# Products without use in TensorE's waits: norms, RWKV projections and latent attention of a two-block network

## The chip, the cores and the metric

One core of one Trainium2 chip runs the whole kernel. The metric is the device time of one execution in microseconds (us); the time quoted is the median of several runs. A profiled execution is a single one, and its trace gives when each instruction ran on each engine: TensorE (PE; its weight loads PEld), VectorE (DVE), ScalarE (ACT), GpSimd (POOL) and the queue that issues most transfers (SP). The trace also gives the TensorE clock that was granted: 1.00 stands for 2.4 GHz, 0.50 for 1.2 GHz, and a value between is a mean over a stretch in which both occurred.

## The reference, cut to what matters

256 tokens of 1024 features (and 256 context tokens) pass through two networks in float32. The first has two layers: a mixer of neighbourhood attention and mLSTM, an MLP, an RWKV-7 mixer, an MLP. The second has two layers of SwiGLU, a mixer (the second one is multi-head latent attention), cross attention to a memory, SwiGLU. The parts that the change touches:

```python
def rms_norm(x, eps=NORM_EPS):
    xf = x.astype(jnp.float32)
    return (xf * lax.rsqrt(jnp.mean(xf * xf, axis=-1, keepdims=True) + eps)).astype(x.dtype)
...
def rwkv_prepare(h, mu, w_rkv, w0, w1, w2, a0, a1, a2, g1, g2, k_k, k_a):
    xx = centred_shift(h) - h
    xr, xw, xk, xv, xa, xg = h[None] + xx[None] * mu[:, None, None, :]
    r, k, v = jnp.einsum('sbtd,sde->sbte', jnp.stack([xr, xk, xv]), w_rkv)
...
def _mla_mixer(h, positions, w_in, q_lora_g, kv_lora_g, w_uq, w_ukv, q_g, k_g, w_out):
    c_q, c_kv, k_r = jnp.split(h @ w_in, [MLA_Q_LORA, MLA_Q_LORA + MLA_KV_LORA], axis=-1)
    q = (_rmsnorm(c_q, q_lora_g) @ w_uq).reshape(b, s, MLA_HEADS, MLA_QK)
    kv = (_rmsnorm(c_kv, kv_lora_g) @ w_ukv).reshape(b, s, MLA_HEADS, MLA_NOPE + MLA_V)
```

## The kernel before, in words

Weights and activations are kept with features on the 128 partitions. Each float32 weight tile is split on the fly into a rounded part (`wh`, by ACT) and a remainder (`wl`, by DVE), and each product is the sum of two or three matmuls (`mm2`, lines 166 to 171; `mm3`, lines 159 to 164). Most of the time TensorE works through such products without a break.

**Norms.** The sum of squares of x is gathered by ACT and DVE (`sumsq`, L262) or ACT and POOL (`pre_norm`, L530), reduced over the partitions by two small matmuls (`rstd_from`, L280), raised to the power -1/2 by POOL (L259), and spread over the partitions again by two matmuls against a diagonal (`bcast_tok`, L290). In `modulate` (L1464) and `rwkv_in` (L2067) these matmuls come ahead of the products that use the norm; in `mla_mixer` (L894) the scale is applied later, but the small matmuls still stand ahead of the products. `modulate` is called with one stream (`len(xs) == 1`) in one place only, the MLP of the first network's second layer (`mlp`, L1964, with `ns == 1`).

**Order of the work.** Outside the planned parts the framework orders the instructions of each engine by itself. Three parts are ordered by hand with a planner, `Weave` (L321): `rwkv_in`, the RWKV scan (`rwkv_scan`, L2561) and `mla_mixer`. Each piece of work is a generator that announces an engine and an estimated duration before it issues instructions (`yield "PE", 0.43`); the planner lets the generators run in the order of estimated start and rank, and that order is what each engine's queue gets. Resources such as PSUM banks are slots that are taken and given back (`take`, `give`): "G" are the four banks pG of the large products, "L" the banks pL of the small ones.

**Warm products.** The planner can put matmuls of the identity with itself, whose output nobody reads, into TensorE's queue. Before each PE piece it adds up what its plan holds for TensorE in the window that ends with this piece, and if that is under the share `DUTY` it adds products ahead of the piece (`keep`, L419). A fourth value of a PE request says what share of its duration counts as load; without it, all of it counts:

```python
    def keep(self, end, work, after=None):
        need = self.DUTY * self.WINDOW - self.load(end) - work
        if need > 0:
            n = math.ceil(need / 0.107)
            self.add_warm(end if after else max(self.free.get("PE", 0.0), end - self.WINDOW), min(n, 4) if after else n, after)
```

One unit of n is 64 columns, up to four units make one matmul call of 256 columns, and the plan's time for PE is moved on by 0.107 us for each unit. Before the change only the scan does this (`rw_warm`, L2751, into a bank pX of its own; `rw_heat`, L2761, 12 such calls ahead of its first work). In `rwkv_in` (L2087) and `mla_mixer` (L944) the line `w.FILL = w.DUTY = 0.0` turns it off.

**rwkv_in** (L2067). After the norms, a front makes the shifted and mixed inputs on DVE, ACT and POOL (`ri_front`, `ri_mix`), and `ri_products` runs the products k, w, a, g, r and v through the banks pG. While r and v run, `ri_items` and `ri_unit` work out decay, a, kk and so on for 8 blocks of features in 2 directions, each with small PE pieces: `ri_low` (L2402, L2403), the spread of kk's scale (L2452) and the sum for the bonus (L2531). The sums of squares of k (L2276) and their transposition (L2359) belong here too. DVE, ACT and POOL work alongside, and SP stores and loads pieces in DRAM.

**mla_mixer** (L894). Products "in", "uq", "ukv" and "out" (`ml_tokens`, `ml_main`) go through pG; norms, rotations, transposes (L1109, L1158, L1232) and attention per head lie between them, and the products of the next stage (`ml_memory`) fill in.

## Time and profile before

| | |
|---|---|
| median of 3 runs | 2817.14 us (2816.12 to 2821.49) |
| the profiled execution, its own time | 2816.91 us |
| span of its trace, first to last instruction | 2814.8 us |
| mean granted TensorE clock over the span | 0.966 |
| PE busy | 2623.0 us (93%) |
| DVE busy | 1898.6 us (67%) |
| ACT busy | 1353.7 us (48%) |
| POOL busy | 401.0 us (14%) |
| chain that ended last | PE 74%, DVE 15%, ACT 4%, POOL 2%, DMA 2% |

The first line is what is to be predicted. The trace describes the profiled execution alone, and its span leaves out about 2 us of start and end. "Busy" of PE counts matmuls at either clock, so that a matmul at 1.2 GHz counts twice as long as the same one at 2.4 GHz. The stages that the change touches lie at 783 to 1057 us (`rwkv_in`), 1373 to 1563 us (the MLP with one stream) and 2361 to 2520 us (`mla_mixer`).

### The profile page before, as it was taken

What the parts mean: (1) busy time and instruction counts of PE and PEld (TensorE: products, weight loads), DVE (VectorE), ACT (ScalarE), POOL (GpSimd) and SP (SyncE); (2) the same over time, 40 slices, a digit from 0 to 9 for tenths busy, and PEclk for the clock granted to TensorE, in tenths of its full rate; (3) what the DMA queues carried; (4) which work ended last, traced back from release to release, by engine and by line L of the source; (5) the groups of instructions that cost most, each with busy time, mean ns of one, the idle gap of its engine ahead of it and who ended that gap; (6) DMA issues with size and microseconds to landing.
All of it is one profiled execution on the core that took longest, in us unless ns stands there. A gap on an engine that the chain in (4) does not pass through costs nothing.

```text
span 2814.8 us, 47376 instructions
## 1 busy us (share of the span) xinstructions
PE 2623.0 (93%) x18980; PEld 2193.8 (78%) x18980; DVE 1898.6 (67%) x3252; ACT 1353.7 (48%) x2548; POOL 401.0 (14%) x396
## 2 busy tenths in 40 slices
PE   6999999999979988886899999999999999799999
PEld 4977667888857675775688888988888888788887
DVE  4463667544376884986785787876876776765884
ACT  3344333223245550676454554554654554664563
POOL 1210100000043552234100101001101001311100
PEclk9999999999988899999899999999999999999999
DMA  7244445533222666232355455533555555233454
GB/s 278 75 158 148 143 150 194 180 120 106 90 73 94 213 226 158 64 81 88 123 195 193 166 182 197 184 124 115 180 190 185 180 190 180 83 121 120 167 193 150
DMA packets 108122, 425.93 MB, mean 151 GB/s; under 512 B 14334, under 2 KB 50430, under 8 KB 66046
## 3 DMA queue, kind: packets, MB, share of 16 engines
q1 hardware_dynamic: 107326, 420.76, 44.3%
q8 instruction: 149, 2.44, 0.4%
q10 hardware_dynamic: 576, 2.15, 0.2%
q14 instruction: 71, 0.58, 0.1%
HBM read 397.68 MB, written 24.13 MB: 150 GB/s over the span
## 4 chain that ended last, share of the span: by engine, by line
PE 74%; DVE 15%; ACT 4%; POOL 2%; issue 2%; DMA 2%; SPq 0%; POOLq 0%; ACTq 0%; DVEq 0%
PE g L170 17%; PE g L171 9%; PE g L162 8%; PE g L163 7%; PE g L164 7%; PE a L170 6%; PE a L171 3%; DVE pr L2736 2%; DVE N L2738 2%; PE pG L162 2%; PE pG L163 2%; PE pG L164 2%; PE d L1405 1%; PE pX L2754 1%; DVE wl L72 1%
## 5 line engine op out<-in xcount | busy, mean ns | idle before, releaser
L72 DVE TENSOR_TENSOR wl<-raw,wh 128x1024 fp32r<-128x1024 f32 x512 | 627.6, 1226 | 359.7 <-ACT wh L71 356.8
L71 ACT CAST wh<-raw 128x1024 fp32r<-128x1024 f32 x512 | 537.1, 1050 | 631.8 <-PE g L170 259.1
L170 PE MATMUL g<-xnh,wh 128*128 128x512 f32 x800 | 287.3, 399 | 5.4 <-DVE xnh L200 5.4
L170 PE MATMUL a<-xnh,wh 128*128 128x512 f32 x704 | 251.9, 397 | 0.0
L170 PE MATMUL g<-hh,wh 128*128 128x512 f32 x704 | 246.6, 396 | 0.0
L171 PE MATMUL g<-xnh,wl 128*128 128x256 f32 x800 | 224.0, 280 | 0.0
L171 PE MATMUL a<-xnh,wl 128*128 128x256 f32 x704 | 197.0, 280 | 0.0
L171 PE MATMUL g<-hh,wl 128*128 128x256 f32 x704 | 196.4, 279 | 0.0
L547 POOL TENSOR_TENSOR acc<-acc,sq 128x256 f32<-128x256 f32 x63 | 65.7, 1042 | 839.9 <-ACT sq L546 561.9
L170 PEld LDWEIGHTS g<-xnh,wh 128*128 128x128 f32 x800 | 150.7, 188 | 42.7 <-DVE xnh L200 4.6
L170 PEld LDWEIGHTS a<-xnh,wh 128*128 128x128 f32 x704 | 132.6, 188 | 31.6
L170 PEld LDWEIGHTS g<-hh,wh 128*128 128x128 f32 x704 | 132.1, 188 | 31.8
L171 PEld LDWEIGHTS g<-xnh,wl 128*128 128x128 f32 x800 | 151.3, 189 | 0.1
L2754 PE MATMUL pX<-ident 128*128 128x256 f32 (+3 forms) x388 | 103.8, 378 | 35.5 <-DVE N L2738 19.2
L163 PE MATMUL g<-wl,hh 128*128 128x256 f32 x448 | 129.3, 289 | 6.6 <-DVE wl L72 6.6
L162 PE MATMUL g<-wh,hh 128*128 128x256 f32 x448 | 131.8, 295 | 3.3 <-ACT wh L71 3.1
L171 PEld LDWEIGHTS a<-xnh,wl 128*128 128x128 f32 x704 | 133.0, 189 | 0.1
L171 PEld LDWEIGHTS g<-hh,wl 128*128 128x128 f32 x704 | 132.6, 188 | 0.0
L164 PE MATMUL g<-wh,hl 128*128 128x256 f32 x448 | 128.5, 287 | 0.0
L259 POOL TENSOR_TENSOR rs<-ms,mhalf 128x2 f32<-128x2 f32 (+2 forms) x53 | 56.5, 1067 | 426.6 <-DVE ms L257 426.5
L2754 PEld LDWEIGHTS pX<-ident 128*128 128x128 f32 x388 | 64.8, 201 | 55.9 <-DVE N L2738 28.8
L162 PE MATMUL g<-hh,wh 128*128 128x512 f32 x256 | 101.1, 397 | 1.5 <-ACT hh L1485 1.5
(635 smaller groups left out, 6995.3 us busy)
## 6 DMA issues: line engine op xcount, KB each, us to landing
raw<-in_w_mlp SPq DMA_DIRECT2D x64, 1024.0 KB, 4.8
raw<-in_w_ada SPq DMA_DIRECT2D x48, 1024.0 KB, 6.4
raw<-in_w_pre_gu SPq DMA_DIRECT2D x44, 1024.0 KB, 4.8
raw<-in_w_post_gu SPq DMA_DIRECT2D x44, 1024.0 KB, 4.8
raw<-in_w_pre_down SPq DMA_DIRECT2D x22, 1024.0 KB, 4.8
raw<-in_w_post_down SPq DMA_DIRECT2D x22, 1024.0 KB, 4.8
raw<-in_w_ab SPq DMA_DIRECT2D x14, 1024.0 KB, 4.9
d_bk<-h SPq DMA_DIRECT2D x16, 512.0 KB, 3.0
```

The lines of the kernel that those rows point to most:

```text
L71: nc.scalar.copy(h[:, :w], r)
L72: nc.vector.tensor_tensor(l[:, :w], r, h[:, :w].bitcast(F32), op=ALU.subtract)
L162: mm(ps, wh, xh, start=start, stop=False)
L163: mm(ps, wh, xl, start=False, stop=False)
L164: mm(ps, wl, xh, start=False, stop=stop)
L170: mm(ps, wh, x, start=start, stop=False)
L171: mm(ps[:, 0], wl, x[:, 0], start=False, stop=stop)
L259: nc.gpsimd.tensor_tensor(rs[:, :n], ms[:, :n], self.mhalf[:, :n], op=ALU.pow)
L547: nc.gpsimd.tensor_tensor(acc, acc, sq, op=ALU.add)
L2736: nc.vector.tensor_tensor(pr, bc(N[:, k + 1 :, k], 2, k), bc(N[:, k, :k], 1, m), op=ALU.mult)
L2738: row = nc.vector.tensor_tensor(N[:, k + 1 :, :k], N[:, k + 1 :, :k], pr, op=ALU.add)
L2754: mm = self.nc.tensor.matmul(o, self.ident, bc(self.ident[:, :64], 1, cols // 64), start=True, stop=True)
```

## The change

A method `idle_products` issues n products of the identity with itself into a PSUM tile that nobody reads. It is called in three norms: 6 products in `mla_mixer` ahead of `rstd_from`; 4, 3 and 7 in `modulate` with one stream, ahead of `rstd_from`, ahead of `bcast_tok` and behind it; 7 and 3 in `rwkv_in`, ahead of `rstd_from` and of `bcast_tok`. In the plans of `rwkv_in` and `mla_mixer` DUTY becomes 0.55 (FILL stays 0), with `wv_warm` as the routine that issues a product: it writes into the bank pG that was handed back last, if the plan has one free at that time, and issues nothing otherwise. `rwkv_in` also gets 12 products of 256 columns at the start of its plan (`wv_heat`). Five PE pieces of `rwkv_in` get another planned duration, and a share of it that counts as load: L2276, L2359, `ri_low`, L2452 and L2531.

```diff
+    def idle_products(self, n):
+        o = self.pst.tile([P, 512], F32, name="t")[:, :T]
+        for _ in range(n):
+            self.nc.tensor.matmul(o.rearrange("p (n t) -> p n t", t=64), self.ident, bc(self.ident[:, :64], 1, 4), start=True, stop=True)
...
+    def wv_warm(self, cols, after=None):
+        now = self.weave.free.get("PE", 0.0)
+        free = [q for at, q in self.weave.slots["G"] if at <= now]
+        if free:
+            o = self.pG[free[-1]][:, :cols].rearrange("p (n t) -> p n t", t=64)
+            self.nc.tensor.matmul(o, self.ident, bc(self.ident[:, :64], 1, cols // 64), start=True, stop=True)
+
+    def wv_heat(self, n):
+        for _ in range(n):
+            yield "PE", 0.427, 0.0
+            self.wv_warm(256)
...
                 self.xn = xh, xl, acc = self.pre_norm(pn, self.vec("mix_norm", 1))
+                self.idle_products(6)
                 self.rs = self.rstd_from(acc, D)
...
                     w = self.weave = Weave(G=4, T=2, S=1, A=1, tmp=2, rop=1, sc=5, pT=4, mq=2, mj=1)
-                    w.FILL = w.DUTY = 0.0
+                    w.FILL, w.DUTY, w.warm = 0.0, 0.55, self.wv_warm
...
         accs = self.sumsq(ph.pools["acc"], [lambda k, x=x: x[:, k] for x in xs], KT)
         more(steps[0])
+        idle = (4, 3, 7) if len(xs) == 1 else (0, 0, 0)
+        if idle[0]:
+            self.idle_products(idle[0])
         rs = [self.rstd_from(acc, D) for acc in accs]
         more(steps[1])
+        if idle[1]:
+            self.idle_products(idle[1])
         rbs = [self.bcast_tok(r, ph.pools["rb"]) for r in rs]
-
+        if idle[2]:
+            self.idle_products(idle[2])
         more(steps[2])
...
-            w.FILL = w.DUTY = 0.0
+            w.FILL, w.DUTY, w.warm = 0.0, 0.55, self.wv_warm
             rm = self.rm = self.phase("rm", acc=2, rb=2, c=1)
             rm.__enter__()
             accs = self.sumsq(rm.pools["acc"], [lambda k, x=x: x[:, k] for x in self.xs], KT)
+            self.idle_products(7)
             rs = [self.rstd_from(acc, D) for acc in accs]
+            self.idle_products(3)
             rbs = [self.bcast_tok(r, rm.pools["rb"]) for r in rs]
...
             w.add(self.ri_rest(enter), 0)
+            w.add(self.wv_heat(12), -1)
...
-            yield "PE", 0.8
+            yield "PE", 0.8, 0.15, 0.2
             for t in range(4):
                 nc.tensor.matmul(self.pK[:, t * 16 + 2 * n : t * 16 + 2 * n + 2], self.os[q][:, t * P : (t + 1) * P], self.hm, start=True, stop=True)
...
-            yield "PE", 0.4
+            yield "PE", 0.7, 0.15, 0.2
             for t in range(4):
                 nc.tensor.matmul(self.pM[r, t * P : (t + 1) * P], rn[:, 16 * t : 16 * t + 16], self.ident, start=True, stop=True)
...
-        yield "PE", 0.43
+        yield "PE", 0.9, 0.15, 0.7
         nc.tensor.matmul(self.pL[g], lr["w"][:, c], lr["h"][z], start=True, stop=False)
...
-            yield "PE", 0.85
+            yield "PE", 0.55, 0.15, 0.15
             nc.tensor.matmul(self.pL[g], self.sel[r, k % 2], self.rT[r], start=True, stop=True)
...
-        yield "PE", 0.4
+        yield "PE", 0.4, 0.15, 0.2
         for t in range(2):
             c = z * 32 + t * 16
             nc.tensor.matmul(self.pM[:, c + k : c + 16 : KT], a[:, t * P : (t + 1) * P], self.hmk[:, k], start=True, stop=True)
```

## Rows read from the trace of the kernel before

**Rows 1.** Windows: the stages touched. Columns as in the head line.
```profile
core 0: us, PE busy (x) PEld busy (x) DVE busy (x) ACT busy (x) POOL busy (x), PEclk, DMA share, GB/s
783.00:833.00 50.00, 29.76 (x112) 23.32 (x112) 44.34 (x62) 23.70 (x41) 24.34 (x20) 0.77 0.15 53
875.00:1057.00 182.00, 161.50 (x879) 128.02 (x879) 145.59 (x183) 97.92 (x160) 97.43 (x96) 0.83 0.55 187
1373.00:1563.00 190.00, 182.49 (x1028) 158.37 (x1028) 134.68 (x213) 95.48 (x149) 0.71 (x1) 0.96 0.53 182
2361.00:2520.00 159.00, 138.72 (x1045) 128.15 (x1044) 109.54 (x273) 92.64 (x216) 39.37 (x25) 0.96 0.35 109
```

**Rows 2.** Windows: five stretches of rwkv_in at the low clock.
```profile
879.00:892.00 13.00, 12.38 (x55) 11.72 (x55) 10.73 (x22) 7.85 (x15) 8.03 (x6) 0.51 0.15 64
897.50:905.50 8.00, 7.23 (x27) 4.52 (x27) 2.14 (x6) 2.27 (x5) 0.00 (x0) 0.57 0.27 115
929.70:939.60 9.90, 9.73 (x20) 4.83 (x21) 9.87 (x11) 5.96 (x11) 7.21 (x8) 0.50 0.58 211
959.60:972.60 13.00, 13.00 (x35) 7.83 (x35) 11.69 (x14) 4.95 (x8) 7.10 (x9) 0.52 0.51 179
...
1024.00:1032.00 8.00, 7.74 (x31) 6.12 (x31) 6.21 (x8) 4.08 (x6) 5.06 (x6) 0.57 0.85 252
```

**Rows 3.** Timeline, PE, rwkv_in: start, us, line, tiles, shape [idle before <- releaser].
```profile
786.40 1.87 PE L280 MATMUL t<-ones,acc 128*128 128x1 f32 x8 [3.61 <-DVE acc L273]
788.92 2.07 PE L290 MATMUL t<-dg,ones 128*128 128x128 f32 x8 [0.66 <-DVE dg L289]
798.29 0.80 PE L162 MATMUL pG<-mh,wh 128*128 128x512 f32 x1 [7.30 <-ACT mh L2201]
...
898.27 1.56 PE L2359 MATMUL pM<-ident,rn 128*16 128x128 f32 x8 [3.35 <-ACT o L2361]
```

**Rows 4.** Timeline, PE, the scan: products of the kind added, 256 columns.
```profile
1341.04 1.56 PE L2754 MATMUL pX<-ident 128*128 128x256 f32 x6
```

**Rows 5.** Timeline (two rows), source L2531 and groups of ACT from 925 to 1048.
```profile
893.98 0.50 PE L2402 MATMUL pL<-lhw,lww 128*128 128x512 f32 x1
894.41 0.50 PE L2403 MATMUL pL<-llw,lww 64*128 64x512 f32 x1
...
L2531 PE MATMUL pM<-hmk,xx x52: 165/251/373, 953.9 to 1051.2; 128*128 128x2 f32 x52
...
L2302 ACT COPY o<-pG 128x512 f32<-128x512 f32 (+1 forms) x14 | 6.6, 488 | 9.6 <-PE pG L164 9.6
```

**Rows 6.** Timeline, PE, the norm of the MLP with one stream.
```profile
1375.17 0.61 PE L280 MATMUL t<-ones,acc 128*128 128x1 f32 x4 [2.07 <-DVE acc L273]
1377.14 1.22 PE L290 MATMUL t<-dg,ones 128*128 128x128 f32 x4 [1.36 <-DVE dg L289]
1381.62 0.80 PE L170 MATMUL g<-x,wh 128*128 128x512 f32 x1 [3.26 <-ACT wh L71]
...
1384.42 0.63 PE L170 MATMUL g<-x,wh 128*128 128x512 f32 x1
...
1390.18 0.40 PE L170 MATMUL g<-x,wh 128*128 128x512 f32 x1
...
1390.53 0.40 PE L170 MATMUL g<-x,wh 128*128 128x512 f32 x1
```

**Rows 7.** Latent attention: two rows of the PE timeline, two windows.
```profile
2364.47 0.61 PE L280 MATMUL t<-ones,acc 128*128 128x1 f32 x4 [2.60 <-POOL acc L547]
...
2414.89 1.09 PE L1158 MATMUL pT<-ident,qn 128*96 128x128 f32 x4 [3.75 <-DVE qn L1085]
...
2366.40:2369.70 3.30, 3.30 (x18) 3.30 (x17) 0.34 (x2) 0.39 (x1) 0.57 (x1) 0.50 0.93 327
2414.80:2421.00 6.20, 6.11 (x29) 6.03 (x30) 2.34 (x6) 1.37 (x2) 0.00 (x0) 0.50 0.48 156
```

**Rows 8.** Timeline, PE, the norm of a SwiGLU stage: order in the queue.
```profile
1571.72 0.80 PE L170 MATMUL g<-xnh,wh 128*128 128x512 f32 x1 [2.56 <-DVE xnh L200]
...
1573.18 1.01 PE L280 MATMUL t<-ones,acc 128*128 128x1 f32 x4
```

## The prediction

> **What bounds the kernel now.** The page comes first: PE is busy for 93% of the span and makes up 74% of the chain that ended last, yet its mean granted clock is 0.966. A busy PE that runs at 1.2 GHz does half the work, so the next view is the table of windows by stage [rows 1]. It shows where clock is missing: 0.83 in the main part of `rwkv_in`, 0.77 in its front, 0.96 in the MLP with one stream and in the latent attention. The reader is to see in the same rows whether a faster PE could be used at all. In the front DVE is busy 44.34 of 50 us and PE 29.76: PE waits there, and its clock costs nothing. From 875 to 1057 PE is busy 161.50 of 182 us and DVE 145.59: both are near their limit. In the MLP (182.49 of 190) and the latent attention (138.72 of 159) PE leads.
>
> Third, windows around the low stretches [rows 2] and the timeline of PE show what came before each fall: a wait, such as 3.35 us for ACT ahead of L2359 [rows 3], or, as at 959.60, small matmuls of little work while PE counts as busy throughout.
>
> **What one product costs.** The scan already issues the same instruction. Three products show as six instructions, 1.56 us together at the full clock [rows 4], so 0.52 us each with the tail, 1.56/3; in a chain a product is planned at 0.427 us, four units of 0.107, and I take 0.43. At the low clock the double, 0.86. No transfer is added, and SP, POOL, ACT and DVE get no instruction.
>
> **Norm of the latent attention, 6 products.** 6 x 0.43 = 2.6 us go into a wait of 2.60 us for POOL's sum [rows 7], which covers them. If that cover were shorter, L280 and all behind it would be late by at most one product, 0.5. Without them the clock fell at 2366.40 and stayed at 0.50 for 3.30 us, with PE busy for all of it and DVE for 0.34. Had it stayed at full clock, the same work would take 1.65 us. Gain 1.6 us; bounds 0 (it falls anyway) and 1.65.
>
> **Norm of the MLP, 4, 3 and 7 products.** They are 1.7, 1.3 and 3.0 us against waits of 2.07, 1.36 and 3.26 us [rows 6]; all fit, and what ends each wait (DVE's sum, the diagonal, the split weights of ACT) does not depend on them. From 1384.42 to 1390.18 nine pairs of L170 and L171 ran, 0.64 us each; the next pair took 0.35 (1390.18 to 1390.53). Nine times 0.29 is 2.6 us. The inputs of the last feature blocks are made by DVE at the same time and would hold PE up a little: I take 2.3, between 0 and 2.6. After that the stage is PE's, so this stays.
>
> **Start of rwkv_in, 7, 3 and 12 products.** 3.0 us go into a wait of 3.61; 1.3 into one of 0.66, which is too short by 0.6; 12 x 0.43 = 5.2 (10.3 at the low clock) into one of 7.30 [rows 3]. The front is DVE's, so a warmer PE gains nothing here. The 0.6 us would delay the spread of the norm, on which the front waits; but L280 ahead of it ran partly at the low clock, 1.87 us for eight, and gets that back. I take 0, between -0.5 and +0.6. If the heat ran cold it would end 3 us late for the first product, which DVE's front hides.
>
> **The plan's load in rwkv_in.** The five stretches [rows 2] lose, each its length times one less its clock, 6.4 + 3.4 + 4.95 + 6.2 + 3.4 = 24.4 us of clock. What is late next is DVE. A faster PE can shorten a stretch at most by what DVE is idle there: 2.3, 5.9, 0.0, 1.3 and 1.8. The smaller of the two, stretch by stretch, is 2.3 + 3.4 + 0 + 1.3 + 1.8 = 8.8 us. The plan sees its own times, not the real waits, and it issues nothing while no bank of pG is free, so I let three quarters of it come: 6.6.
>
> Here a rule of the Trainium skill says more. "TensorE: Matmul & The Clock Gate", section Terms, prices a throttled stretch at its length times one less the clock ratio, whole. By that rule 24.4 instead of 8.8 would be within reach, and the sum below would be 11.7 us lower (three quarters of 15.6); the row of 929.70 [rows 2], in which DVE is busy 9.87 of 9.90 us, speaks against taking all of it.
>
> **Other planned durations.** The plan had 0.43 for `ri_low`; the rows show 0.43 from L2402 to L2403 [rows 5], so some 0.86 for both at the full clock, 32 times: 13.8 us of PE work that the plan did not see. With 0.9 the order of all engines fits better what happens. No row has a price for an order. The nearest is DVE's idle time in 875 to 1057, 36.4 us (182 less 145.59): a better order may take a tenth of it, a worse one add as much. I take a gain of 2, between 4 and -4.
>
> **What the planned products cost.** Where they stand in a real wait they cost nothing. Elsewhere each costs 0.43 us of a PE that is busy 161.50 of 182. I estimate ten of them in `rwkv_in`, 4.3 us, a third of which ends up in the time: 1.5 lost, between 0 and the 22 of the slower rival.
>
> **The plan's load in the latent attention.** PE waited 3.75 us ahead of 2414.89 and then ran 6.20 us at 0.50, while DVE was busy for 2.34 [rows 7]: 3.1 us of clock, on PE's side. The plan may or may not see that wait: half, 1.5. Products in the wrong places, as above, 0.7 lost. Gain 0.8, between 3.1 and -2.
>
> **Sum**, against the profiled execution's own 2816.91 us (its span is 2814.8, and the median of the runs 2817.14, 0.2 away): 1.6 + 2.3 + 0 + 6.6 + 2 - 1.5 + 0.8 = 11.8 us less, 2805.1 us.
>
> **Rivals.**
> - **Everything lost comes back.** If PE's earlier results also move DVE's waits, three quarters of 24.4 (18.3) pass instead of 6.6, and the time is 2805.1 - 11.7 = 2793.4. For it: PE is busy in these stretches for nearly all of their length. Against: so is DVE in two of them [rows 2]. The rule of the Trainium skill named above ("TensorE: Matmul & The Clock Gate", Terms) is on this side.
> - **DVE covers it.** In `rwkv_in` neither the clock nor the new order yields anything, the products cost 1.5, and only the other stages remain (1.6 + 2.3 + 0.8): 2816.9 - 3.2 = 2813.7. For it: DVE's 145.59 of 182 us.
> - **The change does not do what it says in the norms.** Outside the plans PE's queue does not follow the code: in the SwiGLU stage products that use the norm's input came ahead of L280, which stands before them in the code [rows 8]. The idle products depend on nothing but a bank, so they could end up in another place, and the clock would still fall: the 1.6 and 2.3 are gone, 2809.0. Against: in the waits of rows 6 and 7 nothing else was there to run.
> - **Slower.** A planned product writes into the bank that was handed back last. In the real queue ACT may not have read that bank yet, and then PE and all of its queue wait for it: products, `ri_low`, and ACT and DVE behind these. The place is 925 to 1057; one copy out of a bank takes 0.49 us [rows 5], so a misplaced product costs 0.43 + 0.49 = 0.92. The pieces that now count little are 16 groups of L2531 (52 of their 64 instructions are the row in [rows 5]) and 8 of L2452; one product ahead of each makes 24, 22 us, and with all gains above still a loss of 10.3: 2827.2. It decides from 13 such products on (11.8/0.92).
>
> **How the numbers follow.** A measurement of this kernel can tell about 0.2%, 5.6 us, from no change. Chances: forecast 0.46 (its own range 2798 to 2811), everything back 0.17, covered 0.19, moved in the norms 0.06, slower 0.12. Faster by over 0.2% (under 2811.5): nearly all of the forecast, the first rival, most of the moved case and a little of the covered one, 0.70. Within: 0.18, mostly the covered case. Slower: 0.12. The range runs from 2790, a little beyond the first rival, whose 18.3 could be more, to 2821, beyond the covered case with a worse order; what is left out is the slower rival and a sixth or so of the first, under 0.2.
>
> **What would show it.** Right: a granted clock of 0.97 or more from 1373 to 1395 and from 2361 to 2375, with the products as identity matmuls in the waits; in `rwkv_in` a clock of about 0.93 from 875 to its end, and that end some 7 us earlier relative to its start. Wrong: products at a time when PE had work; PE waiting for ACT's copy out of pG ahead of a product; the clock still near 0.5 after small matmuls; or DVE with the same busy time in the same length while the clock is up.

## The result, and the profile after

The changed kernel takes 2829.92 us (median of 5 runs, 2827.5 to 2834.45) against 2816.12 us for the kernel before on the same chip (5 runs, 2808.9 to 2821.49): a ratio of 1.0059, with a 95% interval of 1.0039 to 1.0078. (The ratio, here and below, is the median of the ratios of each run to each run of the kernel before; the two medians alone differ by 13.8 us, the ratio stands for 16.6.) The forecast was 2805.1 us with a range of 2790 to 2821; the change is slower, and its time lies above the range. The profiled execution took 2829.92 us itself, 13.0 more than the one before, with a span of 2828.1 us and a mean granted clock of 0.961 (before 0.966).

The first view is again the table of windows by stage (us from the start, length, busy time of PE, PEld, DVE, ACT and POOL with the number of instructions, granted clock, DMA share, GB/s), with the windows moved along with the work. The third row is the main part of `rwkv_in` cut exactly, from 77 us after its first product to 1 us after the start of its last L2531 (L2560 in the changed file, where the lines behind the first edit are 6 to 29 further down). Between the same two points the kernel before took 176.89 us, at a clock of 0.84.

```profile
776.00:826.00 50.00, 33.88 (x138) 26.43 (x137) 44.06 (x61) 23.66 (x40) 23.81 (x20) 0.85 0.15 49
...
868.00:1067.00 199.00, 178.52 (x937) 140.68 (x936) 144.76 (x191) 99.39 (x161) 90.79 (x89) 0.81 0.50 170
...
868.77:1063.84 195.07, 174.65 (x921) 137.70 (x920) 143.99 (x187) 98.62 (x160) 87.46 (x83) 0.81 0.51 173
...
1384.00:1572.00 188.00, 185.54 (x1058) 160.75 (x1058) 135.15 (x214) 95.56 (x150) 0.71 (x1) 1.00 0.54 186
...
2369.00:2528.00 159.00, 142.91 (x1051) 131.29 (x1050) 107.90 (x270) 90.40 (x212) 38.43 (x25) 0.95 0.35 109
```

Against [rows 1]: the MLP has its full clock (1.00, before 0.96), the latent attention has not gained (0.95, before 0.96), and the main part of `rwkv_in`, which was to gain most, has lost clock (0.81, before 0.83 over the window of [rows 1]) and is 18.2 us longer (195.07 less 176.89), although PE is busier.

To place the rest, DVE's and ACT's unchanged instructions were matched between the two traces (same line, same tile, same count), and the median of their shift was read along the program. Across `rwkv_in` it grows by 16.8 us, across the norm of the MLP it falls by 2.6, and across the latent attention it grows by 2.3. That is 16.5. Of the other 3.5 us, of the opposite sign, 1.1 are gained at the norm of `rwkv_in`, ahead of its first product; the rest comes and goes in code that the change does not touch.

The timeline of PE of the changed kernel (start, us, engine, line, operation, out<-in, shape, count, idle time before it) at the two other norms, MLP first:

```profile
1384.29 1.89 PE L266 MATMUL t<-ident 128*128 128x256 f32 x8
1386.52 0.60 PE L286 MATMUL t<-ones,acc 128*128 128x1 f32 x4 [0.34 <-DVE acc L279]
1386.99 1.54 PE L266 MATMUL t<-ident 128*128 128x256 f32 x6
...
1389.10 3.19 PE L266 MATMUL t<-ident 128*128 128x256 f32 x14
1392.52 0.50 PE L170 MATMUL g<-x,wh 128*128 128x512 f32 x1 [0.23 <-ACT wh L71]
...
2369.73 2.75 PE L266 MATMUL t<-ident 128*128 128x256 f32 x12
2372.50 0.61 PE L286 MATMUL t<-ones,acc 128*128 128x1 f32 x4
2372.97 1.87 PE L525 MATMUL pG<-ident 128*128 128x256 f32 x8
2374.53 0.42 PE L162 MATMUL pG<-wh,xnh 128*128 128x256 f32 x1
```

The idle products (L266) stand where they were meant to, and the waits of [rows 6] shrink from 2.07 and 3.26 us to 0.34 and 0.23. In the latent attention the wait for POOL's sum [rows 7] is filled, but between the norm's small matmuls (L286) and the first product (L162) there are now 8 instructions that the plan put in (L525). Before, that gap (2364.47 to 2364.94) was 0.5 us; now it is 2.0.

The same view in `rwkv_in`:

```profile
780.97 1.05 PE L286 MATMUL t<-ones,acc 128*128 128x1 f32 x8 [0.60 <-DVE acc L279]
...
783.26 1.18 PE L296 MATMUL t<-dg,ones 128*128 128x128 f32 x8
791.77 0.80 PE L162 MATMUL pG<-mh,wh 128*128 128x512 f32 x1 [7.33 <-ACT mh L2230]
...
890.01 4.10 PE L525 MATMUL pG<-ident 128*128 128x256 f32 x10 [5.92 <-ACT o L2356]
894.04 1.89 PE L2388 MATMUL pM<-ident,rn 128*16 128x128 f32 x8
```

The norm's small matmuls (L286, L296) are shorter than before, 1.05 and 1.18 us against 1.87 and 2.07 [rows 3], and the first product follows the first of them after 10.80 us instead of 11.89. The wait of 7.3 us at the front [rows 3] is as empty as before: none of the 12 heat products is there. At 890.01 PE has stood for 5.92 us for ACT's reading of a pG bank (L2356, a tanh) ahead of a planned product, and then runs ten instructions of planned products for 4.10 us at the low clock. In all, 56 such instructions (28 products) lie in `rwkv_in`, and they are busy for 21.79 us.

The end of the stage, in the chain that ended last (start, us, what):

```profile
1053.43 0.59 ACT o L2331
1054.03 0.04 issue
1054.07 4.10 PE pG L525 x10
1058.18 0.75 PE pM L2560 x4
1058.93 3.62 PE pG L525 x8
1062.55 0.66 PE pM L2560 x4
...
1064.04 1.53 DMA d_cf<-cf
```

The last two groups of small sums (L2560), on which a store and then the loads of the scan wait, each stand behind a group of planned products, 7.7 us together.

### The profile page after: what moved, and what is told of

It is laid out like the page before. It is cut to its first block, busy times and chain, and to the rows that moved or that the text cites. A ratio compares the mean times of both kernels' runs of the same rounds, so it can differ in the third digit from the quotient of the medians.

```text
span 2828.1 us, 47621 instructions
## 1 busy us (share of the span) xinstructions
PE 2658.3 (94%) x19110; PEld 2227.8 (79%) x19110; DVE 1895.5 (67%) x3256; ACT 1353.4 (48%) x2548; POOL 395.2 (14%) x392
## 4 chain that ended last, share of the span: by engine, by line
PE 75%; DVE 15%; ACT 4%; POOL 2%; issue 2%; DMA 2%; SPq 0%; ACTq 0%; POOLq 0%; DVEq 0%
PE g L170 17%; PE g L171 9%; PE g L162 8%; PE g L164 7%; PE g L163 7%; PE a L170 6%; PE a L171 3%; PE pG L162 2%; DVE N L2767 2%; DVE pr L2765 2%; PE pG L163 2%; PE pG L164 2%; PE pX L2783 1%; PE d L1425 1%; DVE wl L72 1%
## 5 line engine op out<-in xcount | busy, mean ns | idle before, releaser
L170 PE MATMUL a<-xnh,wh 128*128 128x512 f32 x704 | 251.8, 397 | 0.0
L162 PE MATMUL g<-wh,hh 128*128 128x256 f32 x448 | 131.2, 293 | 3.3 <-ACT wh L71 3.1
L2783 PEld LDWEIGHTS pX<-ident 128*128 128x128 f32 x388 | 69.5, 212 | 44.6 <-DVE N L2767 16.5
L162 PE MATMUL g<-hh,wh 128*128 128x512 f32 x256 | 100.9, 396 | 1.5 <-ACT hh L1511 1.5
```

The lines of the kernel that those rows point to most:

```text
L162: mm(ps, wh, xh, start=start, stop=False)
L170: mm(ps, wh, x, start=start, stop=False)
L2783: mm = self.nc.tensor.matmul(o, self.ident, bc(self.ident[:, :64], 1, cols // 64), start=True, stop=True)
```

## The experiments

Two measures are used. The ratio is that of the times to those of the kernel before on the same chip. The **end of rwkv_in** is read from the timeline: from the start of its first product (L162) to the start of its last product or of its last L2531, whichever is later. A single run of the kernel before varies by 20 us or more (on one chip 35 of them lay between 2801.96 and 2822.2), so both are needed; the two columns of the end come from one profiled execution each. All runs together:

| run | what rwkv_in has | products issued there | last product, us | last L2531, us | ratio, 95% interval |
|---|---|---|---|---|---|
| before | | 0 | 245.6 | 252.9 | 1 |
| e4_norms | nothing new but the norms' products | 0 | 246.5 | 254.8 | 0.9997 [0.998, 1.0014] |
| e3_norms_mla | the same, and load in the latent attention | 0 | 243.9 | 252.2 | 1.0005 [0.9991, 1.002] |
| e12_mla_seed | as e3 | 0 | 243.9 | 251.9 | 1.0001 [0.9984, 1.0018] |
| e6_kk_price | price of L2452's pieces 0.55 | 0 | 250.4 | 252.3 | 0.9999 [0.9986, 1.0013] |
| e7_turn_price | price of the turns (the transpositions, L2359) 0.7 | 0 | 246.3 | 254.0 | 0.9998 [0.9979, 1.0018] |
| e14_heat | heat really issued | 12 | 248.0 | 256.1 | 1.0006 [0.9987, 1.0024] |
| e15_low_06 | `ri_low` at 0.6 | 0 | 250.4 | 251.6 | 0.9987 [0.9969, 1.0006] |
| e17_low_06_again | the same kernel as e15 | 0 | 251.3 | 252.5 | 1.0001 [0.9977, 1.0025] |
| e18_best | `ri_low` at 0.6, and load in the latent attention | 0 | 251.8 | 253.0 | 0.9987 [0.9967, 1.0007] |
| e16_mla_seed | as e3 | 0 | 245.9 | 254.3 | one run only, no ratio |
| e5_low_price | `ri_low` at 0.9 | 0 | 262.0 | 253.4 | 1.0024 [1.0009, 1.0038] |
| e1_no_load | all new prices | 0 | 262.0 | 259.5 | 1.0034 [1.0017, 1.0052] |
| e9_silent | all, load counted, products left out | 0 | 259.3 | 264.8 | 1.0038 [1.0022, 1.0055] |
| e10_no_tail | all but the last 9 products | 19 | 262.3 | 268.3 | 1.0057 [1.0039, 1.0075] |
| e11_oldest_bank | all, other bank | 28 | 262.0 | 268.3 | 1.0056 [1.0031, 1.0081] |
| after | all | 28 | 261.2 | 271.1 | 1.0059 [1.0039, 1.0078] |
| e2_old_prices | load, old prices | 7 | 245.9 | 253.7 | 1.0001 [0.9984, 1.0019] |
| e8_shares | load, old durations, new shares | 22 | 256.3 | 256.6 | 1.0059 [1.0038, 1.0081] |
| e13_shares_again | the same kernel as e8 | 22 | 270.2 | 270.6 | 1.007 [1.0044, 1.0096] |

**1. Load, prices, or neither.** Four kernels, made from the changed one by taking parts back:

```diff
-            w.FILL, w.DUTY, w.warm = 0.0, 0.55, self.wv_warm
+            w.FILL, w.DUTY, w.warm = 0.0, 0.0, self.wv_warm      # e1, in rwkv_in
-        yield "PE", 0.9, 0.15, 0.7
+        yield "PE", 0.43                                         # e2, and the four other prices
```

e3 takes back both and the heat, e4 also the load in the latent attention.

> The changed kernel with the plan's load in rwkv_in set to 0; the prices of the PE pieces, the norms' products and the latent attention stay. Theory A (the planned products of rwkv_in, with the 5.9 us for which PE stood for ACT ahead of one, cost most of the loss): the delay that grew from -6 to +10 us over rwkv_in is mostly gone, about 2815 us, PE waits for ACT ahead of no product, and the wait of 5.92 us is not there. Theory B (the new prices reorder the queues for the worse): still about 2830 us, with the loss along rwkv_in as in the changed kernel. Theory C (the reorder and the products share it): 2820 to 2826 us.

> The changed kernel with the old prices and with the plan's load kept in both stages. Theory A (products): about 2830 us, or more, since with the old prices each small piece counts as full work and fewer products are planned: between 2818 and 2830 us. Theory B (prices): 2813 to 2816 us. Theory C: 2820 to 2826 us.

> The kernel before with the norms' products and the load in the latent attention alone (rwkv_in has neither load, heat nor new prices). Both theories A and B: rwkv_in as long as before, so what is left is the gain of the MLP's norm (2 us) and the change of the latent attention, read from the shift of unchanged instructions as +2 us: 2816 us, within 3 us of the kernel before. If the loss is of another place (the phase of the clock in unchanged code): 2822 us or more.

> The norms' products alone, no load in either stage, old prices. From the shifts: 2 us less in the MLP's norm, 1.6 us less at the start of the latent attention (PE at full clock after the 6 products, and no products of the plan between the norm's sum and the first product): 2812 to 2814 us, 2 to 4 us less than the run with the load in the latent attention. If the norms give nothing that lasts: as the kernel before, 2816 us.

Measured: 1.0034, 1.0001, 1.0005 and 0.9997. The loss is all in `rwkv_in`, since without the new prices and the load there nothing is lost. More than half of it stays when no product is planned (theory A alone falls; 1.0034 is in the range of theory C, though its interval reaches the 1.005 of theory B), and it is gone when the load meets the old prices; but there only 7 products are planned, so this run alone doesn't clear the products.

**2. Which price.** On the base of e4 one duration each; and, on the changed kernel, the old durations with the new shares.

```diff
-        yield "PE", 0.43
+        yield "PE", 0.9                  # e5, ri_low, 32 pieces
-            yield "PE", 0.85
+            yield "PE", 0.55             # e6, L2452
-            yield "PE", 0.4
+            yield "PE", 0.7              # e7, the turns
-        yield "PE", 0.9, 0.15, 0.7
+        yield "PE", 0.43, 0.15, 0.7      # e8, and 0.7 to 0.4, 0.55 to 0.85
```

> The run with the norms' products alone (0.9997 of the kernel before), and in rwkv_in one price more: ri_low at 0.9 in place of 0.43 (32 pieces). The three changed durations together cost 0.0029 of the time (1.0034 without the load, against 1.0005 without load and prices), 8 us. Theory P1 (ri_low's price is the one that spoils the order, since it adds 15 us of planned PE time): 1.0025 or more. Theory P2 (the shorter price of the kk pieces does it): 0.9997. Theory P3 (each new order is as likely better as worse, no single price): something between, with an rwkv_in that differs in other places than that of the run with all three.

> The same base, with the price of L2452's pieces alone changed, 0.85 to 0.55. Between 925 and 960 us their rows show 0.94 us each at a clock of 0.5 to 1.0, so the shorter price is further from what happens, and the plan then puts more of these 16-row products side by side. P1: 0.9997. P2: 1.0025 or more, with a lower granted clock from 925 to 960 us than the base. P3: between.

> The same base, with the price of the turns (L2359, 4 pieces) alone changed, 0.4 to 0.7. Four pieces only: P1 and P2 expect no change, 0.9997 and within 0.001 of it; P3 lets even this move rwkv_in by some us either way.

> The changed kernel with the old durations of all PE pieces but the new shares, which only the load reads: the small pieces count little, so the plan issues more products than with old prices, in the old order. With the old prices whole the load cost nothing (1.0001), with the new ones 0.0025 (1.0059 against 1.0034). If the number of planned products is what costs: 1.003 to 1.005. If the load only costs in the order that the new durations make: 1.000 to 1.001.

Measured: 1.0024, 0.9999, 0.9998 and 1.0059. `ri_low`'s price alone costs most of what the durations cost together, and its end of the stage, 262.0 us, is that of e1. But it is the truer price: at the full clock one of its two matmuls starts 0.43 us after the other [rows 5]. How a truer number can cost is seen in the number of products done. Windows of the first 180 us after the first product, for L162 alone (length, busy time and number, clock, DMA share, GB/s), before and with the price 0.9:

```profile
798.29:978.29 180.00, 74.28 (x200) 0.84 0.35 119
```

```profile
794.93:974.93 180.00, 68.39 (x181) 0.81 0.35 118
```

19 products fewer. The end of the same kernel, e5, in PE's timeline:

```profile
1047.99 0.61 PE L2559 MATMUL pM<-hmk,h 128*128 128x2 f32 x4 [0.33 <-DVE h L2555]
...
1056.89 0.28 PE L164 MATMUL pG<-wh,ml 128*128 128x256 f32 x1
...
1072.04 1.22 PE L2782 MATMUL pX<-ident 128*128 128x256 f32 x2 [8.40 <-DMA we<-d_q]
```

The last small sums start at 1047.99, and products alone run on for 8.9 us; the scan's loads wait for them. In the kernel before it is the other way round: the last product starts at 245.6, the last sum at 252.9. The products (rank 3) get what the plan believes is left of PE beside the small pieces (rank 0). That believed rest got smaller, and the products piled up at the end.

With the same idle time and the same clock of PE, the stage takes equally long whatever stands at its end, so the pile alone does not explain the loss. The main part, from 77 us after the first product to 1 us after the start of the last instruction of the stage, PE alone, shows what was added: e4, then e5.

```profile
871.25:1050.00 178.75, 156.04 (x865) 0.84 0.54 187
```

```profile
871.93:1057.90 185.97, 165.97 (x870) 0.79 0.53 180
```

PE does not stand idle for longer (22.7 us in e4, 20.0 in e5). It is busy for 9.9 us more with nearly the same instructions, at a lower clock: length times one less clock is 28.6 us in e4 and 39.1 in e5. In e1, also without products and with 0.9, it is 37.2 (186.00 us at 0.80). So the price shifts what ends the stage, and its cost is clock that PE lost in the new order. Each is a single execution, and why this order has less clock is not shown.

**3. The products themselves.** On the changed kernel:

```diff
-            w.FILL, w.DUTY, w.warm = 0.0, 0.55, self.wv_warm
+            w.FILL, w.DUTY, w.warm = 0.0, 0.55, lambda cols, after=None: None    # e9
         if free:
+            self.warmed = getattr(self, "warmed", 0) + 1
+        if free and not 19 < self.warmed <= 28:                                  # e10
-            o = self.pG[free[-1]]
+            o = self.pG[free[0]]                                                 # e11
```

> The changed kernel with the plan of rwkv_in exactly as it is, the load counted in its times, but none of the 28 planned products issued there. What is left against the run without the load (1.0034) is the order that the counted load makes; what is missing against the changed kernel (1.0059) is the work of the products themselves. Theory W (the products' own time on PE costs, above all 5.9 us of waiting and 4.1 of products at 884 to 894 and 7.7 us of products ahead of the last L2531 pieces): 1.002 to 1.0035, and a stage whose end comes 10 us or more earlier against its start than in the changed kernel. Theory O (the order that the counted load makes costs): 1.005 to 1.006.

> The changed kernel without the last 9 of the 28 planned products of rwkv_in (the 10 and the 8 instructions at 1054.07 and 1058.93 us, 4.10 and 3.62 us, that stand ahead of the last two groups of L2531 on the chain that ended last). Theory W: 7.7 us less, unless the last groups wait for DVE instead; 1.003 to 1.004, with the gap between the last product of mm3 and the loads of the scan shorter by 5 to 7.7 us. If the tail is covered by another chain (DVE's last factors, the stores): no change, 1.0055 to 1.006.

> The changed kernel, with each planned product written into the bank that was handed back longest ago instead of last. If the wait of 5.92 us for ACT's reading is due to the choice of the bank: PE waits for ACT ahead of the first group of products for less than 1 us, and 0 to 6 us come back (1.004 to 1.0055). If what PE then waits for next is the same Tanh's result (the turns behind it also need ACT): the wait only moves to L2359, and the time stays at 1.0059.

Measured: 1.0038, 1.0057 and 1.0056. Leaving out the 28 products with the plan unchanged gives back 0.0021, about 6 us, and 6.3 us of the end of the stage (264.8 against 271.1). That lies between the ranges of theories W and O and in neither. The intervals of e9 and of the changed kernel overlap; that the three kernels with products in the new order have 1.0056 to 1.0059 and the two without 1.0034 and 1.0038 makes the cost of the products likely. The load's order without them costs about what the prices cost (1.0034). Leaving out only the last 9 gives nothing that the time shows, though the chain of the changed kernel runs through them for 7.7 us: PE then waits for DVE there. Its waits from 776 to 1080 us in e10 (what waited for what: us, times, longest), where the changed kernel has 5.3 us, 2 times, for the same pair between 776 and 1070:

```profile
PE pM L2562 <- DVE xx L2558: 9.7, 5, 3.1
```

By the stage's end 2.8 of the 7.7 us come back, and no more. With the other bank (e11) the wait of 5.92 us is gone, the ten instructions run at the full clock in 2.06 us, and then the turns behind them wait:

```profile
886.74 2.06 PE L525 MATMUL pG<-ident 128*128 128x256 f32 x10
888.73 1.05 PE L2388 MATMUL pM<-ident,rn 128*16 128x128 f32 x8
...
895.01 1.35 PE L2388 MATMUL pM<-ident,rn 128*16 128x128 f32 x7 [3.19 <-ACT o L2390]
```

The kernel before has that wait too, 3.35 us [rows 3]. The bank only moved a wait; its choice is not the cause.

**4. The same queues twice.** The time of e8 (1.0059) and its own profile (the end of the stage only 3.7 us later than before) did not agree, so it ran again, without an edit.

> The kernel with the old durations and the new shares once more, unchanged (its first runs gave 1.0059 [1.0038, 1.0081], while its profiled execution has a stage only 3 us longer than that of the runs without load). If the products cost as they do in the changed order (19 of them 3.5 us of the stage, 5.3 us of the time): about 1.002. If the first measurement holds: 1.004 or more, and the lost time should show in this profile, in rwkv_in or behind it.

Measured: 1.007, and this time the profile shows it. Four windows of e8 and of e13, PE alone (length, busy time and number, clock, DMA share, GB/s), and below them the main part of the stage with all engines:

```profile
880.00:890.00 10.00, 6.65 (x32) 0.67 0.01 2
...
930.00:940.00 10.00, 10.00 (x38) 0.81 0.61 206
940.00:950.00 10.00, 9.52 (x62) 1.00 0.73 222
...
970.00:980.00 10.00, 9.70 (x61) 0.94 0.63 229
...
869.34:1049.97 180.63, 162.25 (x908) 130.19 (x909) 144.93 (x181) 98.06 (x160) 100.44 (x88) 0.86 0.55 185
```

```profile
880.00:890.00 10.00, 3.75 (x29) 0.98 0.11 16
...
930.00:940.00 10.00, 10.00 (x18) 0.50 0.50 188
940.00:950.00 10.00, 10.00 (x59) 0.79 0.43 146
...
970.00:980.00 10.00, 10.00 (x25) 0.50 0.50 174
...
869.28:1063.87 194.59, 173.56 (x908) 136.06 (x909) 146.22 (x182) 98.35 (x160) 99.01 (x88) 0.80 0.50 172
```

The instructions and their order are the same, the first product starts 0.06 us apart, and the ends differ by 14 us. At 880 PE was at a lower clock in e8 (0.67 against 0.98), so that nearly the same instructions (32 and 29) kept it busy for longer; in e13 it was done earlier, stood longer for ACT ahead of the planned products (5.9 us against 2.8), and from 930 on the clock is at half where it was not in e8. With these products the stage was seen to go two ways, and the medians suggest that the long way is the usual one. Without products the five executions with the old order (before, e3, e4, e12, e16) end within 2.9 us of each other, at 251.9 to 254.8. So the load with the new shares (22 products) also costs 16 us or more in the old order: the two causes don't add up, the price alone is enough for about half of the loss, the load with the new shares for all of it. Whether in the old order it is the products or the counted load was not tried.

**5. What is left of the parts.** Heat into a bank that nothing uses yet, a price between the two, and the latent attention's plan begun with a full history. In e12 the history ended at the plan's time 0, before its first piece; the 8 instructions were still there, and it counts as e3 once more.

```diff
             yield "PE", 0.427, 0.0
-            self.wv_warm(256)
+            o = self.pM[:, :256].rearrange("p (n t) -> p n t", t=64)             # e14
+            self.nc.tensor.matmul(o, self.ident, bc(self.ident[:, :64], 1, 4), start=True, stop=True)
-        yield "PE", 0.43
+        yield "PE", 0.6                                                          # e15
+                    w.busy.append((-3.4, 10.0, 1.0))                             # e16; e12: 0.0 for 10.0
```

> The kernel before with the norms' products and the load in the latent attention, rwkv_in as before, and the latent attention's plan started with its history full, so that it plans no products ahead of its first piece. Theory: the 8 instructions and 1.87 us between the sum's spread and the first product are gone, 0.5 us lie between them as before, and PE is at the full clock there; against the run with the load and an empty history the start is 1.5 us shorter, 0.9990 to 1.0000. If another instruction holds the first product (the split input of ACT or POOL): the gap stays near 2 us.

> The norms' products alone, old prices, no load, and the 12 products at the start of rwkv_in's plan, written into the bank of pM, which nothing uses yet, so that they are really issued (in the changed kernel none is, since all four banks of pG are taken by then). Forecast of the prediction: they fill 5.2 us of the wait of 7.3 us, the first products run at the full clock, and the time does not change, since DVE sets the front: 0.9997, the gap from the first product to the last L2531 as in the base (254.75 us) within 1.5 us. Rival: the faster front brings the stage forward by up to 3 us, 0.9987.

> The norms' products alone and ri_low priced at 0.6. Counted from the first product of rwkv_in, the last product of mm3 starts at 246.5 us with the price 0.43 and at 262.0 with 0.9, the last L2531 at 254.8 and 253.4: the price decides which of the two ends the stage. Theory (the plan gives PE's time to the small pieces that it believes long, and the products pile up at the end): the last product between 248 and 256, the last L2531 at 252 to 254, and a time within 0.001 of the base, 0.9990 to 1.0005. Rival (each plan is another draw): the last product outside 248 to 256, or the last L2531 later than 256.

> The norms' products and the load in the latent attention, with the plan's history held full for its first 10 us (in the earlier try it ended before the plan's first piece, and the 4 products were still there). Theory: no products between the spread of the norm's sum and the first product of the latent attention, which starts 0.5 us behind it instead of 2.0, at the full clock.

The heat (e14) is issued, runs at the full clock, fills the wait but for 2.14 us, and changes no time, 1.0006. Only the first product gains by it: after a wait of 2.56 us for DVE the clock is at 0.50 from 797 to 800 us.

```profile
786.10 5.35 PE L531 MATMUL pM<-ident 128*128 128x256 f32 x24
793.59 0.49 PE L162 MATMUL pG<-mh,wh 128*128 128x512 f32 x1 [2.14 <-ACT mh L2231]
```

With 0.6 for `ri_low` (e15) the last product starts at 250.4 us, inside what the theory of the balance allowed (248 to 256), the last sum at 251.6, a little ahead of it (252 to 254), and 191 products are done in the first 180 us, between 181 and 200. Its time, 0.9987, is just below the 0.9990 to 1.0005 that were expected and can't be told from the base. In e16 the first product of the latent attention follows the norm's sum at once:

```profile
2354.35 2.75 PE L266 MATMUL t<-ident 128*128 128x256 f32 x12
2357.11 0.60 PE L286 MATMUL t<-ones,acc 128*128 128x1 f32 x4
2357.58 0.36 PE L162 MATMUL pG<-wh,xnh 128*128 128x256 f32 x1
```

**6. A version that beats both?** e15 again, and e18, which is e16 with `ri_low` at 0.6.

> The norms' products and ri_low at 0.6, unchanged, once more: the first measurement was 0.9987 [0.9969, 1.0006]. If the balance of products and small pieces is worth what the stage shows (last L2531 at 251.6 us against 254.8, 3 us): 0.9985 to 0.9992 again. If it was chance: 0.9995 to 1.0005.

> The norms' products, ri_low at 0.6, and the latent attention's load with a full history at its start: all that was not seen to cost. As the run before it, 0.9985 to 0.9995; the load in the latent attention gives nothing that a time shows (the shifts across it are within 0.5 us of those without it).

Measured: 1.0001 [0.9977, 1.0025] and 0.9987 [0.9967, 1.0007]. In all three executions with 0.6 (e15 and e17 are one kernel) the last product starts 1.2 us ahead of the last sum, against 7.3 to 8.4 with 0.43 (before, e3, e4, e12, e16) and more than 8 behind it with 0.9 (e5): the price does set which of the two ends the stage. That the balance also gains time is not shown. The shift across `rwkv_in` is -3.2 to -2.6 us in these three, but e12, with the old price, has -2.5; none is faster than the kernel before by more than chance, and 1.0001 is what was expected of e17 if the first measurement was chance. All are clearly faster than the changed kernel.

## Why the prediction was wrong

Two steps failed, both in `rwkv_in`: the clock that the load was to give back, and the order that the truer durations were to improve. Together they were to gain 8.6 us; the stage grew by 16.8. Of the signs that the prediction named, the clock of the two norms came (1.00 in both), and two of the signs of being wrong came in `rwkv_in`: products at a time when PE had work, and PE waiting 5.92 us for ACT ahead of one.

- **The plan's load in rwkv_in (6.6 us gained): the first step that failed.** It took the clock as something that products return, and capped it by DVE's idle time. The clock did not come back: length times one less clock, the main part lost 28.3 us of clock before (176.89 x 0.16) and 37.1 after (195.07 x 0.19). Without any product, but with the new durations (e1), it lost 37.2 too: the loss of clock came with the durations, and the products, 21.79 us of PE, did not undo it. Against e9, where the plan is the same and no product is issued (188.78 us at 0.78, so 41.5), 4.4 us less are lost; but the same queues differ by some 14 us in this figure (e8 25.3, e13 38.9), so that no return of clock is shown. The rival in which everything comes back, and the rule on its side (the Trainium skill, "TensorE: Matmul & The Clock Gate", Terms), was not put to the test there, since the stretches stayed throttled. Where the clock did rise, behind the MLP's norm, the stretch from 1384.42 to 1390.18 [rows 6], at a granted clock of 0.50 before, is priced by that rule at 5.76 x 0.5 = 2.9 us, and 2.6 came in the changed kernel: there the trace is near it.
- **The other durations (2 us gained, between 4 and -4): the second step that failed, wrong by sign and outside the bounds.** `ri_low`'s price alone costs 0.0024 to 0.0027 of the time, 7 us, and 6.8 us of shift across the stage. The step "with 0.9 the order of all engines fits better what happens" failed: one truer price took PE's time away from the products in the plan, they were left over at the end, and PE was busy for 9.9 us more with the same work at a lower clock (0.79 against 0.84, e5 against e4). The bound, a tenth of DVE's idle time, looked at DVE, while it was PE's busy time that grew.
- **The planned products (1.5 us lost, between 0 and 22): the number and the length were off, the share near.** 28 were issued in `rwkv_in`, not ten, and at 0.78 us each, not 0.43, most of them ran at the low clock. Leaving them out gives back about 6 us, so a quarter to a third of their 21.79 us ended up in the time, near the third that was taken; with intervals that overlap, this share is no more than likely.
- **The slower rival (2827.2)** came within 3 us of the time, and the wait for ACT that it named is there. That the number fits is luck, as its mechanism is not shown: with another bank the wait goes and the time stays (e11), and without the 9 products ahead of the last small sums it stays too (e10).
- **Norm of the MLP (2.3 gained): right at the norm, and kept in half of the executions.** 2.6 in the changed kernel, and between 1.6 and 2.9 in each of the 18 other executions that have the products. But the step "so this stays" holds in ten of the 19 only. In the other nine (e4 and e17 among them) 2.7 to 3.3 us are lost again, evenly, by the end of the stage, at the full granted clock (see the last section).
- **Norm of the latent attention (1.6) and its load (0.8): the first right at its place and mostly not kept, the second wrong, and the two were not priced together.** In the nine executions without products of the plan at that place the start is 1.9 us shorter in seven, 1.6 and 0.1 in the others. But in seven of the nine the clock falls to half 11 to 16 us behind the norm's sum instead (in e4 it is 0.66 from 2372 to 2377, with PE busy for all of it), and e4 is then only 0.3 us ahead; where it does not fall (e5, e17), 1.7 us stay. The lower bound "it falls anyway" is what mostly happened. With the load and an empty history the plan issues four products right behind the norm, and it is 0.4 shorter to 1.3 longer. Over the whole stage the shift is +1.8 us on average with them (ten executions, -0.5 to 3.1) and -0.5 without (nine, -2.2 to 1.6).
- **Start of rwkv_in (0, between -0.5 and +0.6): outside its bounds by a little, and wrong in what happens.** All 19 executions with the norms' products gain 1.1 us from the norm's first small sum to the first product (11.89 us before, 10.79 to 10.81 in them): ahead of the first product the warmer PE does count, in the small matmuls. The prediction said of the load that it issues nothing while no bank of pG is free, and did not say it of the heat, for which it holds from the first moment: the first four products have taken all four. With a bank of its own the heat changed no time (e14), as forecast: it is hidden by DVE's front.

What stays open: why the order with the truer price has less clock, why the stage goes the long way so often once products are in it, and, as said above, whether in the old order it is the products or the counted load that costs.

## What to carry to other kernels

Products that warm TensorE did no harm where a wait is seen and nothing else is in the queue, as in a norm, though what they gained did not show in the time (0.9997); put in by a plan that doesn't know the real waits, they land ahead of pieces that are ready, and took PE's time without a return of clock that could be seen. Correcting one estimate of a planner that was balanced by its errors can cost more than it gives: count, along the stage, how far each kind of work has come, see which of them is left at the end, and read the clock beside PE's busy time. A gain of clock at one place counts only if it is still there at the end of the stage. And an instruction can only be hidden in a wait if the bank that it asks for is free when it is planned.

## What was not expected of the hardware

The same queues gave two lengths of one stage, 256.6 and 270.6 us (e8 and e13), with a granted clock of 0.86 and 0.80: in the longer one a wait was 3 us longer, and the clock was at half in stretches that lie tens of us behind it; that the wait is the cause is not shown. The profile of a single execution, by which the prediction priced its clock, is one draw of such a stage. And ten instructions of the same product took 4.10 us right after a wait of 5.92 us and 2.06 us without one: products that come after the wait pay the low clock themselves.

At the full granted clock, too, TensorE was seen at two paces. In the MLP with one stream the same stretch of 600 instructions, PE alone, takes 104.00 us in e15 and 106.00 us in e17, which are one program:

```profile
1403.40:1507.40 104.00, 104.00 (x602) 1.00 0.56 191
```

```profile
1403.19:1509.19 106.00, 106.00 (x602) 1.00 0.55 188
```

PE is busy throughout and the clock is 1.00 in both. The kernel before and ten of the 19 others have the shorter time there, nine the longer; what sets it is not shown. The gain at the norm ahead of this stretch is of the same size.
